# Row statistics from the transposed input, and index weights in other slots of the arena

## The chip, the cores and the metric

The kernel runs on one core of a Trainium2 chip. The metric is the device time of one execution in microseconds (us): the median of three runs is 1517.07 us (1515.85 to 1518.37). The core has an engine for matrix products (TensorE, PE in the views), whose weight loads are listed apart (PEld), VectorE (DVE), ScalarE (ACT), GpSimd (POOL) and SyncE (SP), which issues most transfers. Each engine works through its own list of instructions in order and waits for others by semaphores. SBUF holds the tiles, PSUM the products.

## What is computed

One layer of a streaming encoder on 1024 rows of width 1024 in float32. The start, on which the change bears, is this; the three mixers, the gates and the channel mixer follow and are only named here.

```python
def rms_norm(x, g):
    y = x32 * lax.rsqrt(jnp.mean(x32 * x32, axis=-1, keepdims=True) + EPS)
    return y * g

h = rms_norm(x, g_mix[l])
z = h @ w_in[l]
aq, ak, av, bq, bk, bv, iq, ik, iw, cx, cy, gt = split_cols(z)
q_i = apply_rope(iq, cos, sin)                      # the indexer: 4 heads of 64
k_i = apply_rope(rms_norm(ik, g_idx_k[l]), cos, sin)
dots = jnp.einsum('bqhe,bse->bqhs', qib, ki)
score = jnp.einsum('bqhs,bqh->bqs', jax.nn.relu(dots), wib)
# top 256 keys by score for branch B; y_a, y_b, y_c; gates; w_out; SwiGLU with w_ffn_in, w_ffn_out
```

The mean of squares is over the width of a row, so each of the 1024 rows has one scale.

## The kernel before, in words

Precision is kept by splitting each float32 operand in two parts: `split` (L100) rounds on ScalarE (`hi`, L101) and subtracts on VectorE (`lo`, L102), and `mm3` (L116) makes three products of them (L117 to L119). The normalized input is kept transposed, width on the partitions, as eight pairs of tiles `hTh` and `hTl`, one for each 128 of the width, 1024 rows long.

The rows come in five batches, `BATCH` (L29): one tile of 128 rows, one, and three times two. Per batch the queue of SyncE loads the rows themselves (`x`, 512 KB a tile, L166), for their sums of squares, and the same rows transposed (`xT`, 512 KB each, L172), for the products. Behind the first batch stand the small parameters (`sm`) and the index weights in three pieces of two, three and three chunks (`W0K`, L146, L150); behind the last the rope table (`cs`). These loads are kept in program order. Then, per batch: ScalarE squares each row tile and adds along the row (L187), GpSimd multiplies and adds epsilon (`rs_v`, L126) and raises to the power of -0.5 (`rs_x`, L127), TensorE transposes a broadcast of that column so that the scale of each row lies along the free axis of a PSUM bank (`rb`, L190), and VectorE multiplies eight chunks by gain and scale (L197); each of the eight is split, where the first batch also splits the index weights at chunks 0, 2 and 5. The index projection (L254 to L262) is 24 products for each of eight row tiles, 192 in all, 324 columns each. After four tiles the index keys are normalized (`ssk`, `rsk`), queries and keys are rotated (L279 to L286) and transposed (L291, L295), and for blocks 2 to 7 of 128 queries the scores are made: two products for each head (L242, L243), relu on ScalarE (L310), weighted sums on VectorE (L312, L314). Beside that the first projections of the other branches run (`w_zg`, tiles `wzr`, `wzh`, `wzl`, products of 256 columns in L117 to L119).

Tiles come from two lists of arena slots: `ring` (slots 0 to 6) for weights that stream through, among them the index weights and `w_zg`, and `sl` (slots 7 to 49) for the rest. A slot that was freed goes to the end of its list, and a tile in it waits for the readers of the tile before. What stands where in the list of each engine is decided by a scheduler from the program text and the tiles' dependences; only loads marked as kept in program order, and a string of letters for the work further behind, fix places by hand.

Of the kernel before, what the change touches and what calls it, by code (L numbers as in the profile page):

```python
# [10 lines left out]
F32 = mybir.dt.float32  # L11
F32R = mybir.dt.float32r
I32 = mybir.dt.int32
BF16 = mybir.dt.bfloat16
AF = mybir.ActivationFunctionType
OP = mybir.AluOpType
# [4 lines left out]
D = 1024  # L21
NT = 8
KD = 8
DFF = 2816
NF = DFF // 128
EPS = 1e-6
# [53 lines left out]
def hybrid_kernel(ctx: ExitStack, tc: tile.TileContext, x, xt, small, cs, bias_a, lru_w, w_idx, w_zg, w_c, w_g, w_b,  # L80
                  w_o, w_fi, w_fo, out):
    nc = tc.nc
    V, S, G, PE = nc.vector, nc.scalar, nc.gpsimd, nc.tensor
    const = ctx.enter_context(tc.tile_pool(name="const", bufs=1))
    arena = ctx.enter_context(tc.tile_pool(name="arena", bufs=1))
    dram = ctx.enter_context(tc.tile_pool(name="dram", bufs=1, space=bass.MemoryType.DRAM))
    sl = Slots(arena, range(NRING, NSLOT))
    ring = Slots(arena, range(NRING))
# [7 lines left out]
    def smc(name, j=0, n=1):  # L96
        o, _ = SMALL_OFF[name]
        return sm[:, o + j:o + j + n]

    def split(raw, hi, lo, eng=None):  # L100
        S.activation(hi, raw, AF.Copy)  # L101
        (eng or V).tensor_tensor(lo, raw, hi.bitcast(F32), op=OP.subtract)  # L102
# [13 lines left out]
    def mm3(o, lh, ll, rh, rl, first, last, **kw):  # L116
        PE.matmul(o, lhsT=lh, rhs=rh, start=first, stop=False, **kw)  # L117
        PE.matmul(o, lhsT=lh, rhs=rl, start=False, stop=False, **kw)  # L118
        PE.matmul(o, lhsT=ll, rhs=rh, start=False, stop=last, **kw)  # L119

    mhalf = const.tile([128, 16], F32, name="mhalf")
    V.memset(mhalf, -0.5)

    def rsqrt(dst, src, n, scale):
        v = const.tile([128, n], F32, name="rs_v", tag=f"rsv{n}", bufs=2)
        G.tensor_scalar(v, src, scale, EPS, op0=OP.mult, op1=OP.add)  # L126
        G.tensor_tensor(dst, v, mhalf[:, 0:n], op=OP.pow)  # L127
# [4 lines left out]
    def gbank(shape=(128, 512)):  # L132
        return psum.tile(list(shape), F32, name="G", tag="G", bufs=2)

    def sbank(shape=(128, 1024)):
        return psum.tile(list(shape), F32, name="S", tag="S", bufs=2)

    def tbank(shape=(128, 512)):
        return psum.tile(list(shape), F32, name="T", tag="T", bufs=2)

    ss_x = const.tile([128, NT], F32, name="ss_x")
    rs_x = const.tile([128, NT], F32, name="rs_x")
# [3 lines left out]
    W0K = ((0, 2), (2, 3), (5, 3))  # L146

    def load_w0(k0, kn):
        raw = ring.get((128, kn, 324), F32, "w0r")
        tc.keep_in_program_order(nc.sync.dma_start(raw, w_idx[:, k0:k0 + kn, :]))  # L150
        w0.append([k0, kn, raw])

    def split_w0(q):
        k0, kn, raw = w0[q]
        hi, lo = ring.get((128, kn, 324), F32R, "w0h"), ring.get((128, kn, 324), F32R, "w0l")
        split(raw, hi, lo)
        ring.free(raw)
        w0[q] = (k0, kn, hi, lo)

    xts, parts = [None] * NT, []
    for t0, tn in BATCH:
        for t in range(t0, t0 + tn):
            xts[t] = sl.get((128, D), F32, "x")
            tc.keep_in_program_order(nc.sync.dma_start(xts[t], x[t * 128:(t + 1) * 128, :]))  # L166
        kn = KD // tn
        ps_ = []
        for n in range(tn):
            c0 = 1024 * (t0 + n)  # L170
            pt = sl.get((128, kn, 128 * tn), F32, "xT")
            tc.keep_in_program_order(nc.sync.dma_start(pt.rearrange("p k t -> p (k t)"), xt[:, c0:c0 + 1024]))  # L172
            ps_.append(pt)
        parts.append(ps_)
        if t0 == 0:
            tc.keep_in_program_order(nc.sync.dma_start(sm, small))
            for q in range(len(W0K)):
                load_w0(*W0K[q])
        if t0 == 6:
            ctab = sl.get((128, NT, 2, 64), F32, "cs")  # L180
            tc.keep_in_program_order(nc.sync.dma_start(ctab, cs))
    junk = sl.get((128, D), F32, "junk")
    for (t0, tn), ps_ in zip(BATCH, parts):
        w = 128 * tn
        rb = sbank((128, w))
        for t in range(t0, t0 + tn):
            S.activation(junk, xts[t], AF.Square, accum_out=ss_x[:, t:t + 1])  # L187
        rsqrt(rs_x[:, t0:t0 + tn], ss_x[:, t0:t0 + tn], tn, 1.0 / D)
        for t in range(t0, t0 + tn):
            PE.transpose(rb[:, 128 * (t - t0):128 * (t - t0) + 128], rs_x[:, t:t + 1].to_broadcast([128, 128]), ident)  # L190
        kn = KD // tn
        for k in range(KD):
            if t0 == 0 and k in (0, 2, 5):
                split_w0((k + 1) // 3)
            r = ps_[k // kn][:, k % kn]
            hi, lo = (a[:, 128 * t0:128 * t0 + w] for a in hT[k])
            V.scalar_tensor_tensor(r, r, smc("g_mix", k), rb, op0=OP.mult, op1=OP.mult)  # L197
            split(r, hi, lo)
        sl.free(*xts[t0:t0 + tn], *ps_)
    sl.free(junk)  # L200

    def bc(ap, n):
        a = list(ap.ap)
        return bass.AP(tensor=ap.tensor, offset=ap.offset, ap=[a[0], *a[1:-1], [0, n], a[-1]])
# [44 lines left out]
    for g in range(2):  # L249
        zq = sl.get((128, 4, 4, 64), F32, "zq")  # L250
        zk = sl.get((128, 4, 2, 64), F32, "zk")
        for j in range(4):
            t = 4 * g + j
            p = gbank((128, 324))  # L254
            for k0, kn, wh, wl in w0:
                for k in range(k0, k0 + kn):
                    hh, hl = hT[k]
                    mm3(p, hh[:, 128 * t:128 * t + 128], hl[:, 128 * t:128 * t + 128], wh[:, k - k0], wl[:, k - k0],
                        k == 0, k == KD - 1)
            S.activation(zq[:, j].rearrange("p h d -> p (h d)"), p[:, 0:256], AF.Copy)  # L260
            S.activation(zk[:, j, 0], p[:, 256:320], AF.Copy)
            S.activation(iw[:, t], p[:, 320:324], AF.Copy, scale=1.0 / 16.0)  # L262
        if g == 1:
            for _, _, wh, wl in w0:
                ring.free(wh, wl)
        sq = sl.get((128, 4, 64), F32, "sq")
        S.activation(sq, zk[:, :, 0], AF.Square)
        ssk = const.tile([128, 4], F32, name="ssk", bufs=2)
        V.tensor_reduce(ssk, sq, axis=AX.X, op=OP.add)
        rsk = const.tile([128, 4], F32, name="rsk", bufs=2)  # L270
        rsqrt(rsk, ssk, 4, 1.0 / 64)
        for j in range(4):
            V.scalar_tensor_tensor(zk[:, j, 0], zk[:, j, 0], rsk[:, j:j + 1], smc("gi", 0, 64), op0=OP.mult,
                                   op1=OP.mult)
        sl.free(sq)
        t2 = sl.get((128, 4, 4, 64), F32, "t2")
        ct = ctab[:, 4 * g:4 * g + 4, 0, :]
        st = ctab[:, 4 * g:4 * g + 4, 1, :]
        V.tensor_mul(t2[:, :, :, 0:32], zq[:, :, :, 32:64], bc(st[:, :, 0:32], 4))  # L279
        V.tensor_mul(t2[:, :, :, 32:64], zq[:, :, :, 0:32], bc(st[:, :, 32:64], 4))  # L280
        V.tensor_mul(zq, zq, bc(ct, 4))
        V.tensor_add(zq, zq, t2)
        V.tensor_mul(t2[:, :, 0, 0:32], zk[:, :, 0, 32:64], st[:, :, 0:32])
        V.tensor_mul(t2[:, :, 0, 32:64], zk[:, :, 0, 0:32], st[:, :, 32:64])
        V.tensor_mul(t2[:, :, 1], zk[:, :, 0], ct)
        V.tensor_add(zk, bc(t2[:, :, 0], 2), bc(t2[:, :, 1], 2))  # L286
        c = slice(512 * g, 512 * g + 512)
        for pr in range(2):
            pt = tbank((128, 4, 128))
            for j in range(4):  # L290
                PE.transpose(pt[:, j], zq[:, j, 2 * pr:2 * pr + 2].rearrange("p h d -> p (h d)"), ident)  # L291
            stack(pt.rearrange("p a b -> p (a b)"), qi[2 * pr][:, c], qi[2 * pr + 1][:, c])
        pt = tbank((128, 4, 128))
        for j in range(4):
            PE.transpose(pt[:, j], zk[:, j].rearrange("p h d -> p (h d)"), ident)  # L295
        pk = pt.rearrange("p a b -> p (a b)")
        S.activation(kih[:, c], pk, AF.Copy)
        V.tensor_sub(kil[:, c], pk, kih[:, c].bitcast(F32))
        sl.free(zq, zk, t2)
# [4 lines left out]
    for i in range(2, NT):  # L304
        w = (i + 1) * 128
# [965 lines left out]
    ring = Slots(arena, fore + rw.free_list + rr.free_list + sl.free_list[:9])  # L1271
# [242 lines left out]
```

## Time and profile before

| | before |
|---|---|
| median of 3 runs | 1517.07 us (1515.85 to 1518.37) |
| profiled execution, its time | 1517.05 us |
| its span | 1515.3 us |
| PE busy | 1469.1 us, 97% of the span |
| VectorE busy | 1119.1 us, 74% |
| ScalarE busy | 762.9 us, 50% |
| GpSimd busy | 109.5 us, 7% |
| TensorE's mean granted clock | 0.994 |

The span is the profiled work from its first to its last instruction; 1.75 us lie around it. A busy share is a mean over stages with different limits, so a stage is read from its own stretch. Times in the views are us from the start of the span. A line of the timeline is one instruction or a run of equal ones: start, time, engine, line, operation, what is written and read, shape, count, and in brackets how long the engine had waited before it and for what. A matmul's time includes its passage through the array; how often one starts is the distance of the starts.

### The profile page before, as it was taken

What the parts mean: (1) busy time and instruction counts of PE and PEld (TensorE: products, weight loads), DVE (VectorE), ACT (ScalarE), POOL (GpSimd) and SP (SyncE); (2) the same over time, 40 slices, a digit from 0 to 9 for tenths busy, and PEclk for the clock granted to TensorE, in tenths of its full rate; (3) what the DMA queues carried; (4) which work ended last, traced back from release to release, by engine and by line L of the source; (5) the groups of instructions that cost most, each with busy time, mean ns of one, the idle gap of its engine ahead of it and who ended that gap; (6) DMA issues with size and microseconds to landing.
All of it is one profiled execution on the core that took longest, in us unless ns stands there. A gap on an engine that the chain in (4) does not pass through costs nothing.

```text
span 1515.3 us, 19935 instructions
## 1 busy us (share of the span) xinstructions
PE 1469.1 (97%) x7556; PEld 1228.5 (81%) x7556; DVE 1119.1 (74%) x1985; ACT 762.9 (50%) x1208; POOL 109.5 (7%) x161
## 2 busy tenths in 40 slices
PE   6999899999999998999999989999999999999999
PEld 5898688989788876788888868888888888888887
DVE  7989999869666779767889776555555556578972
ACT  6557768775778656443214663333333333344340
POOL 1220011210000200110000200000000000000000
PEclk9999999999999999999999999999999999999999
DMA  7011212122111121357552412323232323697532
GB/s 289 29 46 54 87 32 102 39 70 85 56 53 45 42 102 53 125 181 298 216 189 75 153 59 96 111 97 112 98 111 98 111 97 126 230 386 263 190 125 89
DMA packets 52240, 182.59 MB, mean 120 GB/s; under 512 B 6000, under 2 KB 6128, under 8 KB 52144
## 3 DMA queue, kind: packets, MB, share of 16 engines
q1 hardware_dynamic: 38448, 135.17, 25.9%
q0 software_dynamic: 11968, 43.00, 7.2%
q10 hardware_dynamic: 1728, 3.15, 0.5%
q8 instruction: 59, 0.97, 0.3%
q14 instruction: 37, 0.30, 0.1%
HBM read 135.94 MB, written 45.35 MB: 120 GB/s over the span
## 4 chain that ended last, share of the span: by engine, by line
PE 75%; DVE 14%; ACT 5%; issue 3%; DMA 2%; POOL 0%; POOLq 0%; ACTq 0%; SPq 0%; DVEq 0%
PE B L119 15%; PE B L118 15%; PE B L117 15%; PE G L118 7%; PE G L119 7%; PE G L117 6%; DVE key L643 3%; PE T L426 2%; PE T L118 1%; PE T L117 1%; PE T L119 1%; PE T L418 1%; PE S L117 1%; PE S L118 1%; PE S L119 1%
## 5 line engine op out<-in xcount | busy, mean ns | idle before, releaser
L118 PE MATMUL B<-hl,fwh 128*128 128x512 f32 x528 | 205.8, 392 | 1.5 <-DVE hl L1026 1.5
L117 PE MATMUL B<-hh,fwh 128*128 128x512 f32 x528 | 203.4, 393 | 1.6 <-ACT hh L1025 1.3
L119 PE MATMUL B<-hh,fwl 128*128 128x512 f32 x528 | 198.8, 391 | 1.9 <-DVE fwl L102 1.9
L117 PEld LDWEIGHTS B<-hh,fwh 128*128 128x128 f32 x528 | 99.8, 189 | 23.5 <-ACT hh L1025 2.2
L119 PEld LDWEIGHTS B<-hh,fwl 128*128 128x128 f32 x528 | 99.8, 189 | 23.1 <-DVE fwl L102 2.3
L118 PEld LDWEIGHTS B<-hl,fwh 128*128 128x128 f32 x528 | 99.8, 189 | 22.9 <-DVE hl L1026 2.2
L118 PE MATMUL G<-wzl,hTh 128*128 128x256 f32 x384 | 111.3, 290 | 5.3 <-DVE wzl L102 5.3
L117 PE MATMUL G<-wzh,hTh 128*128 128x256 f32 x384 | 110.8, 291 | 1.3 <-ACT wzh L101 0.6
L119 PE MATMUL G<-wzh,hTl 128*128 128x256 f32 x384 | 110.8, 289 | 0.0
L102 DVE TENSOR_TENSOR fwl<-s,fwh 128x1024 fp32r<-128x1024 f32 x44 | 53.7, 1223 | 74.1 <-PE B L118 74.1
L118 PE MATMUL B<-fol,foh 128*128 128x512 f32 x264 | 102.9, 390 | 0.0
L119 PE MATMUL B<-foh,fol 128*128 128x512 f32 x264 | 101.9, 389 | 0.0
L117 PE MATMUL B<-foh,foh 128*128 128x512 f32 x264 | 101.1, 389 | 0.0
L655 ACT ACTIVATE junk_s<-score,ngS 128x1024 int8<-128x1024 f32 (+2 forms) x78 | 77.5, 994 | 17.5 <-DVE ngS L653 13.5
L118 PEld LDWEIGHTS G<-wzl,hTh 128*128 128x128 f32 x384 | 74.6, 194 | 7.1 <-DVE wzl L102 6.1
L119 PE MATMUL G<-hTh,wgl 128*128 128x512 f32 x192 | 75.8, 395 | 2.0 <-DVE wgl L102 2.0
L117 PEld LDWEIGHTS G<-wzh,hTh 128*128 128x128 f32 x384 | 74.6, 195 | 3.2 <-ACT wzh L101 1.1
L117 PE MATMUL G<-hTh,wgh 128*128 128x512 f32 x192 | 75.8, 395 | 0.0
L118 PE MATMUL G<-hTl,wgh 128*128 128x512 f32 x192 | 75.4, 393 | 0.0
L119 PEld LDWEIGHTS G<-wzh,hTl 128*128 128x128 f32 x384 | 74.8, 195 | 0.3 <-issue 0.2
L101 ACT ACTIVATE fw<-fb 128x512 fp32r<-128x512 f32 x22 | 13.9, 632 | 117.0 <-PE B L119 117.0
L101 ACT ACTIVATE foh<-fa 128x1024 fp32r<-128x1024 f32 x33 | 35.0, 1061 | 57.5 <-DMA fa<-pd 37.7
(486 smaller groups left out, 3847.7 us busy)
## 6 DMA issues: line engine op xcount, KB each, us to landing
fw<-in_w_fo SPq DMA_DIRECT2D x33, 512.0 KB, 5.7
fa<-pd SPq DMA_DIRECT2D x33, 512.0 KB, 5.5
gl<-gd SPq DMA_DIRECT2D x24, 512.0 KB, 5.9
fa<-in_w_fi SPq DMA_DIRECT2D x22, 512.0 KB, 3.5
fb<-in_w_fi SPq DMA_DIRECT2D x22, 512.0 KB, 3.6
pd<-act POOLq DMA_DIRECT2D x22, 512.0 KB, 5.3
ga<-in_w_g SPq DMA_DIRECT2D x18, 512.0 KB, 3.6
x<-in_x SPq DMA_DIRECT2D x16, 512.0 KB, 5.9
```

What stands on the lines that cost most here:

```text
L101: S.activation(hi, raw, AF.Copy)
L102: (eng or V).tensor_tensor(lo, raw, hi.bitcast(F32), op=OP.subtract)
L117: PE.matmul(o, lhsT=lh, rhs=rh, start=first, stop=False, **kw)
L118: PE.matmul(o, lhsT=lh, rhs=rl, start=False, stop=False, **kw)
L119: PE.matmul(o, lhsT=ll, rhs=rh, start=False, stop=last, **kw)
L418: PE.transpose(pt[:, b - c0], P[:, 128 * b:128 * b + 128], ident)
L426: PE.matmul(o[64 * e:64 * e + 64, :], lhsT=v[(b0 + b) // 4][:, (b0 + b) % 4, h, :], rhs=PT[e][:, b, :], start=b == 0, stop=b == nb - 1, sk ...
L643: V.tensor_scalar(o[:, 0:(i + 1) * 128], (keys or score)[i], ap[:, j:j + 1], 0.0, op0=op, op1=OP.add, accum_out=self.cnt[:, j:j + 1])
L655: S.activation(junk_s[:, 0:(i + 1) * 128], score[i], AF.Sign, bias=self.ng.bitcast(F32)[:, j:j + 1], accum_out=self.cnt[:, j:j + 1])
```

## The change

The row tiles `x` and their loads in the prologue are gone. Each `xT` tile is squared on ScalarE into a tile `sq` of the same size, and TensorE adds the squares over the partitions: for each row tile eight float32 products, the squares as weights (128x128), a column of ones as the moving side, into a bank of PSUM. VectorE scales this and adds epsilon on its way out of PSUM, and GpSimd only takes the power. The index weights (raw tiles and both parts) take slots of `sl` and no longer of `ring`. Lines behind the change lie 7 further down.

```diff
     def load_w0(k0, kn):
-        raw = ring.get((128, kn, 324), F32, "w0r")
+        raw = sl.get((128, kn, 324), F32, "w0r")
...
         k0, kn, raw = w0[q]
-        hi, lo = ring.get((128, kn, 324), F32R, "w0h"), ring.get((128, kn, 324), F32R, "w0l")
+        hi, lo = sl.get((128, kn, 324), F32R, "w0h"), sl.get((128, kn, 324), F32R, "w0l")
         split(raw, hi, lo)
-        ring.free(raw)
+        sl.free(raw)
...
-    xts, parts = [None] * NT, []
+    parts = []
     for t0, tn in BATCH:
-        for t in range(t0, t0 + tn):
-            xts[t] = sl.get((128, D), F32, "x")
-            tc.keep_in_program_order(nc.sync.dma_start(xts[t], x[t * 128:(t + 1) * 128, :]))
         kn = KD // tn
...
-    junk = sl.get((128, D), F32, "junk")
+    ones = const.tile([128, 1], F32, name="ones")
+    V.memset(ones, 1.0)
     for (t0, tn), ps_ in zip(BATCH, parts):
         w = 128 * tn
+        kn = KD // tn
         rb = sbank((128, w))
-        for t in range(t0, t0 + tn):
-            S.activation(junk, xts[t], AF.Square, accum_out=ss_x[:, t:t + 1])
-        rsqrt(rs_x[:, t0:t0 + tn], ss_x[:, t0:t0 + tn], tn, 1.0 / D)
+        sums = tbank((128, tn))
+        sqs = []
+        for pt in ps_:
+            sq = sl.get((128, kn, w), F32, "sq")
+            S.activation(sq, pt, AF.Square)
+            sqs.append(sq)
+        for t in range(tn):
+            for k in range(KD):
+                PE.matmul(sums[:, t:t + 1], lhsT=sqs[k // kn][:, k % kn, 128 * t:128 * t + 128], rhs=ones,
+                          start=k == 0, stop=k == KD - 1)
+        sl.free(*sqs)
+        V.tensor_scalar(ss_x[:, t0:t0 + tn], sums, 1.0 / D, EPS, op0=OP.mult, op1=OP.add)
+        G.tensor_tensor(rs_x[:, t0:t0 + tn], ss_x[:, t0:t0 + tn], mhalf[:, 0:tn], op=OP.pow)
         for t in range(t0, t0 + tn):
             PE.transpose(rb[:, 128 * (t - t0):128 * (t - t0) + 128], rs_x[:, t:t + 1].to_broadcast([128, 128]), ident)
-        kn = KD // tn
...
-        sl.free(*xts[t0:t0 + tn], *ps_)
-    sl.free(junk)
+        sl.free(*ps_)
...
-                ring.free(wh, wl)
+                sl.free(wh, wl)
```

The order of VectorE's list from the first batch's scale on, before (`xT_102` is the first batch's tile, `xT_113` the second's):

```order
L372 TENSOR_SCALAR ga_824<-sm 128x1
L494 TENSOR_SCALAR hb<-sm 128x8
L495 TENSOR_SCALAR hb<-sm 128x24
L197 SCALAR_TENSOR_TENSOR xT_102<-xT_102,sm,S 128x128 x8
L102 TENSOR_TENSOR w0l_149<-w0r_105,w0h_148 128x648
L102 TENSOR_TENSOR hTl_85<-xT_102,hTh_84 128x128
```

The same place after (`xT_100` is the first batch's tile; `ss_x` is the new instruction that takes the sums out of PSUM):

```order
L379 TENSOR_SCALAR ga_881<-sm 128x1
L501 TENSOR_SCALAR hb<-sm 128x8
L502 TENSOR_SCALAR hb<-sm 128x24
L102 TENSOR_TENSOR w0l_143<-w0r_103,w0h_142 128x648
L102 TENSOR_TENSOR w0l_153<-w0r_105,w0h_152 128x972
L196 TENSOR_SCALAR ss_x<-T 128x1
L102 TENSOR_TENSOR w0l_166<-w0r_107,w0h_165 128x972
L205 SCALAR_TENSOR_TENSOR xT_100<-xT_100,sm,S 128x128 x8
L102 TENSOR_TENSOR hTl_85<-xT_100,hTh_84 128x128
```

The three index splits moved ahead of the first batch's multiplications, and the new instruction stands between the second and the third.

VectorE's list where the third batch begins, before (`xT_119` and `xT_121` are its tiles):

```order
L102 TENSOR_TENSOR hTl_97<-xT_113,hTh_96 128x128
L102 TENSOR_TENSOR hTl_99<-xT_113,hTh_98 128x128
L197 SCALAR_TENSOR_TENSOR xT_119<-xT_119,sm,S 128x256 x4
L197 SCALAR_TENSOR_TENSOR xT_121<-xT_121,sm,S 128x256 x4
L102 TENSOR_TENSOR hTl_85<-xT_119,hTh_84 128x256
L102 TENSOR_TENSOR hTl_87<-xT_119,hTh_86 128x256
```

The same place after (`xT_111` and `xT_113` are the third batch's tiles):

```order
L102 TENSOR_TENSOR hTl_97<-xT_109,hTh_96 128x128
L102 TENSOR_TENSOR hTl_99<-xT_109,hTh_98 128x128
L196 TENSOR_SCALAR ss_x<-T 128x2
L102 TENSOR_TENSOR wzl_892<-wzr_889,wzh_891 128x1024
L102 TENSOR_TENSOR wzl_1118<-wzr_1115,wzh_1117 128x1024
L205 SCALAR_TENSOR_TENSOR xT_111<-xT_111,sm,S 128x256 x4
L205 SCALAR_TENSOR_TENSOR xT_113<-xT_113,sm,S 128x256 x4
L102 TENSOR_TENSOR hTl_85<-xT_111,hTh_84 128x256
L196 TENSOR_SCALAR ss_x<-T 128x2
L102 TENSOR_TENSOR hTl_87<-xT_111,hTh_86 128x256
```

Two differences of `w_zg` now stand ahead of the third batch's multiplications (another stands among the second batch's differences), and the fourth batch's sums are taken out after one difference of the third.

TensorE's list around the transposes of the fourth batch, before (`L190` with x2 is a batch's pair; `w0h`, `w0l` are the index weights' parts):

```order
L117 MATMUL G<-w0h_171,hTh_94 128x324
L119 MATMUL G<-w0h_171,hTl_97 128x324
L190 MATMUL S<-ident,rs_x 128x128 x2
L117 MATMUL G<-w0h_171,hTh_98 128x324
L118 MATMUL G<-w0l_172,hTh_98 128x324
```

TensorE's list after, from the third batch's transposes to the fourth's (`sq_269` and `sq_271` are the fourth batch's squares, `sq_319` and `sq_321` the fifth's; 12 index products stand ahead of the last two rows' transposes):

```order
L193 MATMUL T<-ones,sq_271 128x1
L199 MATMUL S<-ident,rs_x 128x128 x2
L193 MATMUL T<-ones,sq_271 128x1 x3
L193 MATMUL T<-ones,sq_319 128x1 x4
L193 MATMUL T<-ones,sq_321 128x1 x4
L193 MATMUL T<-ones,sq_319 128x1 x4
L193 MATMUL T<-ones,sq_321 128x1 x4
L118 MATMUL G<-w0l_153,hTh_90 128x324
L119 MATMUL G<-w0h_152,hTl_91 128x324
L199 MATMUL S<-ident,rs_x 128x128 x2
L117 MATMUL G<-w0h_152,hTh_92 128x324
```

Before, 16, 32, 85 and 98 of the 192 index products stood ahead of the transposes of batches 1 to 4 (counted from 0); after, 10, 10, 12 and 30.

## Rows read from the trace of the kernel before

**Rows 1.** The page's part 1 (busy us, share of span) and part 4 (chain).

```profile
PE 1469.1 (97%) x7556; PEld 1228.5 (81%) x7556; DVE 1119.1 (74%) x1985; ACT 762.9 (50%) x1208; POOL 109.5 (7%) x161
...
PE 75%; DVE 14%; ACT 5%; issue 3%; DMA 2%; POOL 0%; POOLq 0%; ACTq 0%; SPq 0%; DVEq 0%
```

**Rows 2.** Stretches: length; busy PE, PEld, DVE, ACT, POOL; clock, DMA share, GB/s.

```profile
0.00:25.00 25.00, 14.46 (x68) 12.57 (x69) 16.85 (x66) 17.12 (x47) 5.13 (x15) 1.00 0.94 364
25.00:50.00 25.00, 22.41 (x150) 21.32 (x150) 20.54 (x50) 13.27 (x43) 7.45 (x5) 1.00 0.26 94
...
150.00:200.00 50.00, 41.64 (x242) 33.93 (x241) 48.95 (x169) 33.98 (x68) 1.06 (x2) 0.93 0.21 74
```

**Rows 3.** DMA issues in 0 to 100 us: count, KB, median us to landing.

```profile
x<-in_x SPq DMA_DIRECT2D x8, 512.0 KB, 9.9
xT<-in_xt SPq DMA_DIRECT2D x8, 512.0 KB, 10.2
```

**Rows 4.** Short stretches around the end of the loads, columns as in Rows 2.

```profile
20.00:25.00 5.00, 4.03 (x28) 3.76 (x27) 4.83 (x14) 5.00 (x16) 0.45 (x2) 1.00 1.03 408
25.00:30.00 5.00, 5.00 (x36) 4.99 (x35) 1.82 (x6) 3.07 (x9) 1.58 (x3) 1.00 0.92 365
30.00:35.00 5.00, 4.11 (x26) 3.51 (x24) 5.00 (x14) 4.56 (x16) 0.00 (x0) 1.00 0.01 3
```

**Rows 5.** Timeline of VectorE, 0 to 84 us.

```profile
15.27 2.16 DVE L197 SCALAR_TENSOR_TENSOR xT<-xT,sm,S 128x128 f32<-128x128 f32 x8 [1.62 <-PE S L190]
17.34 1.82 DVE L102 TENSOR_TENSOR hTl<-xT,hTh 128x128 fp32r<-128x128 f32 x8
19.31 3.22 DVE L197 SCALAR_TENSOR_TENSOR xT<-xT,sm,S 128x256 f32<-128x256 f32 x8 [0.15 <-PE S L190]
...
28.65 3.22 DVE L197 SCALAR_TENSOR_TENSOR xT<-xT,sm,S 128x256 f32<-128x256 f32 x8 [3.17 <-PE S L190]
...
38.54 2.76 DVE L102 TENSOR_TENSOR hTl<-xT,hTh 128x256 fp32r<-128x256 f32 x8
41.22 0.68 DVE L280 TENSOR_TENSOR t<-zq,cs 128x512 f32<-128x512 f32 x1
...
53.33 1.23 DVE L102 TENSOR_TENSOR wzl<-wzr,wzh 128x1024 fp32r<-128x1024 f32 x1
...
75.07 0.62 DVE L312 TENSOR_SCALAR score<-relu,iw 128x768 f32<-128x768 f32 x1 [0.45 <-ACT relu L310]
```

**Rows 6.** Timeline of ScalarE, 0 to 10 us.

```profile
4.33 1.06 ACT L187 ACTIVATE junk<-x 128x1024 f32<-128x1024 f32 x1 [2.31 <-DMA x<-in_x]
```

**Rows 7.** Timeline of GpSimd, 0 to 50 us.

```profile
27.29 0.19 POOL L126 TENSOR_SCALAR rs_v<-ss_x 128x2 f32<-128x2 f32 x1 [1.60 <-ACT junk L187]
27.57 0.69 POOL L127 TENSOR_TENSOR rs_x<-rs_v,mhalf 128x2 f32<-128x2 f32 x1
37.10 4.86 POOL L126 TENSOR_SCALAR rs_v<-ssk 128x4 f32<-128x4 f32 x1 [8.85 <-DVE ssk L269]
```

**Rows 8.** Timelines of TensorE's weight loads, 57 to 59.3 and 150 to 160 us.

```profile
57.25 0.46 PEld L295 LDWEIGHTS T<-ident,zk 128*128 128x128 f32 x4
...
151.70 0.41 PEld L426 LDWEIGHTS T<-PT,v 128*64 128x64 f32 x6 [0.35 <-issue]
```

**Rows 9.** Timeline of TensorE, 0 to 75 us.

```profile
14.27 0.47 PE L119 MATMUL G<-w0h,hTl 128*128 128x324 f32 x1
14.54 0.47 PE L117 MATMUL G<-w0h,hTh 128*128 128x324 f32 x1
...
16.34 0.31 PE L117 MATMUL G<-w0h,hTh 128*128 128x324 f32 x1
16.49 0.31 PE L118 MATMUL G<-w0l,hTh 128*128 128x324 f32 x1
...
48.27 1.03 PE L291 MATMUL T<-ident,zq 128*128 128x128 f32 x8
...
54.61 0.39 PE L118 MATMUL G<-wzl,hTh 128*128 128x256 f32 x1 [2.20 <-DVE wzl L102]
...
69.46 0.44 PE L242 MATMUL S<-kih,qi 128*128 128x384 f32 x1 [0.20 <-ACT relu L310]
```

## The prediction

> **What bounds the kernel now.** I read the page's shares first [rows 1]: TensorE is busy 97% of the span and makes up 75% of the chain that ended last, so only its gaps and what stands on its path can pay. The table by stretches says where gaps are [rows 2]: 10.5 us idle in 0 to 25 us, 2.6 in 25 to 50, and 8.4 in 150 to 200, where VectorE is busy 48.95 of 50 us and sets the pace. The change touches only the first 75 us. There the loads come first: xT's tiles of 512 KB take 10.2 us each from issue to landing, as x's eight do [rows 3], and the queue moves 408 GB/s until it has nothing left at about 29.5 us (a share of 0.92 in 25 to 30 us, 0.01 in 30 to 35) [rows 4]. VectorE, which normalizes the five batches of rows, waits 1.62 us before batch 1's multiplications and 3.17 before batch 3's (at 28.65) [rows 5]. So half the x load could go, and these 4.8 us with it. That is what the change can win; what it pays lies in the order of the instructions.
>
> **Removed.** Eight loads of 512 KB are 4,096 of 10,133 KB ahead of and with cs; at 408 KB per us the queue is 10.0 us less full. The squares of row tiles on ScalarE (1.06 us for 128x1024 [rows 6]) are replaced by eight squares of the same size, so ScalarE gets no relief. GpSimd's multiply-add per batch (0.19 us [rows 7]) becomes a VectorE instruction on one or two columns; I take 0.1 us, between 0 and the 0.2 of GpSimd, five times.
>
> **Added on TensorE.** 64 sum products, fp32, 128 weights by one column. An fp32 product shows two weight loads (line 426: the order has 264 products, the trace 528 loads). Six loads of 64 columns take 0.41 us, 0.07 each, and four of 128 take 0.46, 0.115 each [rows 8]. So one product costs at least 0.14 us; with the 128 columns that the weights have here 0.23, and 0.46 if all runs at TensorE's lower clock. I take 0.23, by the row with the same columns: 64 x 0.23 = 14.7 us (9 to 29). Nothing below zero is possible, since nothing is taken from TensorE for it. Most of it falls into times in which TensorE waits anyway; the price is in what stands behind it.
>
> **Moved, and queued.** Three facts of the order decide. (a) On TensorE only 10, 10 and 12 of the 192 index products stand ahead of the transposes of batches 1, 2 and 3; before, 16, 32 and 85 did. TensorE takes its list in order, so 180 index products wait for batch 3's transposes, which wait for GpSimd's power. (b) On VectorE the index weights' second split stands ahead of batch 0's scale; and, the index weights having left the ring, three w_zg tiles load right behind cs and their splits (1.23 us each [rows 5]) stand ahead of batch 2's multiplications. (c) Batch 3's scale stands behind batch 2's multiplications and one difference.
>
> Step by step, by VectorE's durations [rows 5]: eight multiplications 2.16 us (128 columns) or 3.22 (256), eight differences 1.82 or 2.76, a w_zg split 1.23 (an index split is smaller). The power takes 0.69 [rows 7], and from its end at 28.26 to the multiplications at 28.65 pass 0.4 us for the transposes.
> Loads: the first tile lands at about 4.3 us, where ScalarE's first square begins [rows 6]; small and index weights, 1,429 KB, stand behind it. The last xT lands 4,608 KB before the old end, at 29.5 - 4,608/400 = 18.0, the third w_zg tile at 29.5 - 2,560/400 = 23.1.
> *Batch 0.* The second index tile is there 943 KB after the first landing, at 6.6; ScalarE's rounding of it, behind a square (1.06 each), and VectorE's split (up to 1.23) put the scale at about 9.8. The third split ends at 11.1, then power and transpose: multiplications at 12.2.
> *Batch 1.* VectorE: 12.2 + 2.16 + 1.82 + 0.1, power and transpose: 17.4. TensorE's transpose also stands behind ten index products that need batch 0's differences (from 14.6) and six sums; at the lower clock 14.6 + 2.7 + 2.8 + 0.4 = 20.5. So 17.4 to 20.5 (before 15.27).
> *Batch 2.* 2.16 + 1.82 + 0.1 + 3.69 later VectorE is free, at 25.2 to 28.3, and not before the third w_zg tile is rounded and split (23.1 + 1.06 + 1.23 = 25.4). Power and transposes: 26.5 to 29.4 (before 19.31).
> *Batch 3.* 3.22 + 0.34 + 0.1 gives the scale at 30.2 to 33.1. Seven differences behind it take 2.4 us, then the power 0.69: transposes at 33.3 to 36.2, multiplications 0.4 later (before 28.65).
>
> The power's wait in batches 2 and 3 is the step that needs a row [rows 7]: the multiply-add that GpSimd issued at 37.10 took 4.86 us, until 41.96, while VectorE ran one instruction behind the other to 41.22 + 0.68 = 41.90 [rows 5]; beside pauses of VectorE the same takes 0.19. I therefore let a power end 0.69 us after VectorE's next pause.
> The Trainium skill has a rule that says otherwise ("SBUF — State Buffer", section "Who interferes with whom"): a VectorE instruction with two SBUF inputs and a GpSimd instruction that reads SBUF exclude each other, by a lock that is held for one whole instruction. By that the power would slip in between two differences, batch 3 would come some 2 us earlier and the kernel end at about 1526; the row of 4.86 us speaks against it, and "GpSimd is not held" below has its case.
>
> From batch 3's transposes on TensorE has 180 index products, 0.15 us apart (16.34 to 16.49 [rows 9]), 26.7 us, and 1.5 for twelve transposes among them (0.13 each, eight in 1.03): they end at 61.5 to 64.4 instead of 48.27. From there to the first product of block 4's scores passed 69.46 - 48.27 = 21.2 us. Of that go 2.2 us of waiting for a w_zg split (54.61), which the early loads remove, and 1.5 for the twelve transposes that now stand earlier: 17.5; up to 1 us more if the pauses for ScalarE's relu (0.20 at 69.46) shrink. So that product comes at 78.0 to 81.9, 8.5 to 12.4 later. From the fifth score block on, the order on all engines is that of before but for swaps of neighbours; VectorE's first step of block 5 (75.07 before) shifts by the same. TensorE and VectorE are full in turn behind it, so the shift reaches the end. The lower end needs the early value of each step at once, so I take 11: 1517.05 + 11 = **1528 us**. The profiled execution (1517.05) lies 0.02 below the median of 1517.07, so nothing is corrected.
>
> **Rivals.**
> *The lower clock lasts: slower still.* At the start the index products come every 0.27 us (14.27 to 14.54), 324 columns at 1.2 GHz, and from 16.34 every 0.15, near 2.4 GHz [rows 9]. The granted clock of that stretch reads 1.00 [rows 2], so the level is read from the spacing. Now TensorE stands still for some 3 us ahead of batch 2's transposes and again ahead of batch 3's. If some 25 to 30 products behind them run at the lower level, they cost 0.12 more each: +3 to +3.6, with sums at 0.46 up to +8; 1532. For it: sums of one column are little work. Against: they keep TensorE issuing between the waits.
> The Trainium skill ("TensorE: Matmul & The Clock Gate", section "What's actually happening") calls the lower clock the default, which activity lifts; the rise at 16.34 agrees.
> *GpSimd is not held.* The power runs between VectorE's instructions and a sum costs 0.14: batch 2 comes 1.1 us earlier, batch 3 another 2.4, with the lower end of batch 1 about 5 less, 1523. For it: 0.69 at 27.57. Against: the 4.86 row.
> *Faster.* The relief of the queue wins. It decides at batch 3: if its multiplications begin before 28.65, VectorE's 3.17 and 1.62 us of waiting are gone and the order costs nothing: 1517.05 - 4.8 = 1512. It would need sums at the low bound and w_zg splits that don't hold VectorE; their place in its order speaks against it.
> *No change.* The shift is absorbed where TensorE waits 8.4 us, in 150 to 200 us [rows 2]: 1517 to 1519. Against: VectorE is busy 48.95 of 50 us there with work that is itself behind the shifted blocks, so these waits move along.
>
> **How the numbers follow.** 0.2%, 3 us, is about what a measurement of this kernel can tell from no change. The forecast has 0.50 (1528, alone 1525 to 1531), the lower clock 0.22 (1532, to 1536), GpSimd not held 0.13 (1523, from 1520), faster 0.07 and no change 0.08. The range of 1520 to 1536 leaves out the last two. Faster 0.07, same 0.08, slower 0.85.
>
> **What will show it.** In the changed profile: multiplications of batch 0 at about 12.2 us, batch 1 at 17 to 20, batch 2 at 26.5 to 29, batch 3 at 34 to 36.5; GpSimd's powers of batches 2 and 3 longer than 0.69 or begun at VectorE's pauses; TensorE waiting for rs_x ahead of both transposes; a last index product at 61 to 65; block 5's first step on VectorE at 84 to 87, and from there to the end the same time as before. I am wrong if batch 3's multiplications begin before 30 us, if a sum costs far from 0.23 us, or if the time behind block 5 changes by over 2 us.

## The result: 15 us slower, and where the profile shows it

The changed kernel takes 1532.89 us (median of 4 runs, 1531.19 to 1533.18) against 1517.72 before: a ratio of 1.0097, 95% interval 1.0085 to 1.0109, or +15.2 us. The forecast was 1528, the range 1520 to 1536. The direction, the place and most of the size came as foreseen; the wait that makes it is another one. One execution of the run e1 below, 1705.91 us at a mean granted clock of 0.808 where its others have 0.99, is left out.

The page of the changed kernel, part 1 (busy us, share of span, count):

```profile
PE 1490.4 (97%) x7684; PEld 1253.8 (82%) x7684; DVE 1120.2 (73%) x1991; ACT 764.9 (50%) x1200; POOL 109.4 (7%) x156
```

TensorE has 128 more instructions and is busy 21.3 us longer than in [rows 1]; the span is 1531.0 us. Stretches (length; busy PE, PEld, DVE, ACT, POOL; clock; DMA share; GB/s):

```profile
0.00:25.00 25.00, 16.28 (x74) 16.20 (x75) 11.43 (x51) 16.64 (x30) 3.20 (x9) 1.00 0.83 311
25.00:50.00 25.00, 25.00 (x130) 24.94 (x131) 19.26 (x51) 11.33 (x32) 5.12 (x3) 1.00 0.00 1
```

The loads are over before 25 us, as the change meant; in 25 to 50 the queue moves 1 GB/s (before 94 [rows 2]). But TensorE, which before had 2.6 us of gaps there, has none now, and VectorE's idle time went from 4.5 to 5.7 us. Timeline of TensorE (start, time, engine, line, operation, count, idle before and for what):

```profile
5.70 3.57 PE L193 MATMUL T<-ones,sq 128*128 128x1 f32 x16 [5.70 <-ACT sq L189]
12.29 0.48 PE L199 MATMUL S<-ident,rs_x 128*128 128x128 f32 x1 [3.02 <-POOL rs_x L197]
...
21.34 9.81 PE L193 MATMUL T<-ones,sq 128*128 128x1 f32 x46
31.02 0.67 PE L199 MATMUL S<-ident,rs_x 128*128 128x128 f32 x2
31.48 8.11 PE L193 MATMUL T<-ones,sq 128*128 128x1 f32 x38
...
40.13 0.63 PE L199 MATMUL S<-ident,rs_x 128*128 128x128 f32 x2
...
42.72 0.44 PE L119 MATMUL G<-w0h,hTl 128*128 128x324 f32 x1
42.99 0.32 PE L117 MATMUL G<-w0h,hTh 128*128 128x324 f32 x1
...
69.79 0.31 PE L119 MATMUL G<-w0h,hTl 128*128 128x324 f32 x1
```

A product of a sum shows as two records. 46 records take 9.81 us, 38 take 8.11: 0.213 each, **0.427 us a product**, near the 0.46 that the forecast named for the case that all runs at TensorE's lower clock. TensorE stands in sums from 21.34 to 39.45 with nothing else between but two transposes. Batch 2's transposes (31.02) and batch 3's (40.13) come when the sums ahead of them in the list are done; there is no idle time before either (two index products stand ahead of batch 3's). The index products start 0.27 us apart until 42.72 and 0.15 behind 42.99, and end at 69.9 instead of 48.3 [rows 9]. VectorE shows the same from the other side:

```profile
12.81 2.16 DVE L205 SCALAR_TENSOR_TENSOR xT<-xT,sm,S 128x128 f32<-128x128 f32 x8 [1.00 <-PE S L199]
...
21.59 2.16 DVE L205 SCALAR_TENSOR_TENSOR xT<-xT,sm,S 128x128 f32<-128x128 f32 x8 [4.41 <-PE S L199]
...
26.48 2.53 DVE L102 TENSOR_TENSOR wzl<-wzr,wzh 128x1024 fp32r<-128x1024 f32 x2
31.72 3.22 DVE L205 SCALAR_TENSOR_TENSOR xT<-xT,sm,S 128x256 f32<-128x256 f32 x8 [2.71 <-PE S L199]
...
35.27 2.43 DVE L102 TENSOR_TENSOR hTl<-xT,hTh 128x256 fp32r<-128x256 f32 x7
39.62 0.16 DVE L196 TENSOR_SCALAR ss_x<-T 128x2 f32<-128x2 f32 x1 [1.92 <-PE T L193]
40.80 3.22 DVE L205 SCALAR_TENSOR_TENSOR xT<-xT,sm,S 128x256 f32<-128x256 f32 x8 [1.02 <-PE S L199]
...
91.94 0.62 DVE L319 TENSOR_SCALAR score<-relu,iw 128x768 f32<-128x768 f32 x1 [0.46 <-ACT relu L317]
```

Every wait of VectorE just ahead of a batch's multiplications is for TensorE (`PE S`). The first step of block 5, 75.07 before [rows 5], is at 91.94, 16.9 later. Behind it 1439.1 us pass to the end of the span, before 1440.2: the shift is carried, 1.1 us come back. That it is carried through the waits of 150 to 200 us shows when that stretch and the next are read 15.75 us later (first the row of 200 to 400 us of the kernel before, then the two of the changed kernel):

```profile
200.00:400.00 200.00, 197.38 (x1291) 171.96 (x1291) 169.66 (x431) 147.29 (x281) 24.05 (x24) 0.99 0.19 63
```

```profile
165.75:215.75 50.00, 41.77 (x240) 33.76 (x239) 48.95 (x171) 33.59 (x68) 1.60 (x3) 0.93 0.21 74
215.75:415.75 200.00, 197.03 (x1296) 170.98 (x1295) 170.41 (x434) 147.88 (x282) 24.09 (x24) 1.00 0.18 62
```

TensorE is busy 41.77 of 50 us and VectorE 48.95, against 41.64 and 48.95 in [rows 2], and 197.03 of the next 200 against 197.38. The gaps moved with the work; none was used up.

### The profile page after: what moved, and what is told of

It is laid out like the page before. It is cut to its first block, busy times and chain, and to the rows that moved or that the text cites. A ratio compares the mean times of both kernels' runs of the same rounds, so it can differ in the third digit from the quotient of the medians.

```text
span 1531.0 us, 20152 instructions
## 1 busy us (share of the span) xinstructions
PE 1490.4 (97%) x7684; PEld 1253.8 (82%) x7684; DVE 1120.2 (73%) x1991; ACT 764.9 (50%) x1200; POOL 109.4 (7%) x156
## 4 chain that ended last, share of the span: by engine, by line
PE 78%; DVE 13%; ACT 5%; issue 2%; DMA 2%; SPq 0%; POOL 0%; ACTq 0%; DVEq 0%
PE B L119 15%; PE B L118 14%; PE B L117 14%; PE G L118 7%; PE G L119 7%; PE G L117 7%; DVE key L650 3%; PE T L433 2%; PE T L193 1%; PE T L118 1%; PE T L119 1%; PE T L117 1%; PE T L425 1%; PE S L249 1%; PE S L117 1%
## 5 line engine op out<-in xcount | busy, mean ns | idle before, releaser
L662 ACT ACTIVATE junk_s<-score,ngS 128x1024 int8<-128x1024 f32 (+2 forms) x78 | 77.5, 993 | 17.5 <-DVE ngS L660 13.4
L1229 DVE TENSOR_TENSOR act<-act,B 128x512 f32<-128x512 f32 x22 | 15.1, 688 | 65.7 <-PE B L119 65.7
```

Of the source, the lines that this page charges most:

```text
L662: S.activation(junk_s[:, 0:(i + 1) * 128], score[i], AF.Sign, bias=self.ng.bitcast(F32)[:, j:j + 1], accum_out=self.cnt[:, j:j + 1])
L1229: V.tensor_add(a1, a1, x)
```

## The experiments

Two theories. **T**: the shift comes from the sum products, 0.427 us each at the lower clock, that stand in TensorE's list ahead of the transposes of batches 2 and 3. **D**: it comes from VectorE and GpSimd, that is, from the w_zg splits ahead of batch 2's multiplications (which the free ring made possible) and the power that VectorE holds up, the step on which the forecast was built.

From the first step of block 5 to the end of the span it is 1438 to 1446 us in the kernels below, before 1440.2. So the end of a run carries between 2 us less and 6 us more that the prologue's rows don't explain, and the verdicts go by those rows first. The rows are those of one execution each; e8's (1525.88 us) is the fastest of its five and lies 4.3 us under their median.

| kernel | median us | ratio (95%) | batch 3's multiplications | first step of block 5 |
|---|---|---|---|---|
| before | 1518 | | 28.65 | 75.07 |
| changed | 1532.89 | 1.0097 (1.0085 to 1.0109) | 40.80 | 91.94 |
| e1 slots only | 1516.30 | 0.9992 (0.9982 to 1.0001) | 29.04 | 75.06 |
| e2 ring back | 1539.68 | 1.0141 (1.0126 to 1.0156) | 40.18 | 94.93 |
| e3 one-pass sums | 1519.58 | 1.0010 (1.0001 to 1.0020) | behind batch 2's (29.22) | 81.43 |
| e4 idle products | 1541.13 | 1.0150 (1.0135 to 1.0165) | 40.80 | 93.71 |
| e5 extra sums | 1536.10 | 1.0119 (1.0102 to 1.0136) | 33.76 | 93.11 |
| e6 half the sums | 1525.26 | 1.0052 (1.0037 to 1.0067) | 32.27 | 80.05 |
| e7 sums in rows, root | 1523.92 | 1.0037 (1.0024 to 1.0050) | 33.61 | 80.41 |
| e8 sums in a row | 1530.22 | 1.0077 (1.0064 to 1.0091) | behind batch 2's (26.38) | 79.69 |
| e9 e8, ring | 1522.49 | 1.0031 (1.0020 to 1.0042) | 30.74 | 81.12 |
| e10 e8, order held | 1522.04 | 1.0029 (1.0017 to 1.0041) | 31.94 | 76.77 |
| e11 e10, ring | 1526.86 | 1.0058 (1.0046 to 1.0071) | 32.20 | 78.78 |

**e1: the slots alone.** The kernel before with the slots of the change:

```diff
-        raw = ring.get((128, kn, 324), F32, "w0r")
+        raw = sl.get((128, kn, 324), F32, "w0r")
...
-                ring.free(wh, wl)
+                sl.free(wh, wl)
```

> The kernel before with only the index weights moved to the other slots; row tiles and their sums as before. Theory T (the shift of 15 us comes from the 64 sum products, which ran at TensorE's lower clock, 0.427 us each, ahead of the transposes of batches 2 and 3): the prologue has the order of before, so 1516 to 1520. Theory D (the w_zg splits on VectorE and GpSimd's held power set the shift, which the free ring made possible): a good part of the shift is here too, 1521 to 1527.

Nothing: 1516.30, and the first step of block 5 at 75.06. Moving the index weights does no harm by itself; the loss is in the other part or in both together. The run says less on D than its expectation meant: with the loads of `x` still there, the first w_zg split stands behind batch 3's multiplications and not ahead of batch 2's (VectorE):

```profile
40.19 1.22 DVE L102 TENSOR_TENSOR wzl<-wzr,wzh 128x1024 fp32r<-128x1024 f32 x1
```

What splits ahead of batch 2 do is left to e2.

**e2: the ring back.** The changed kernel with that edit undone.

> The changed kernel with the index weights back in the ring, so that no w_zg split stands ahead of batch 2's multiplications; TensorE's list is that of the changed kernel. T: batch 2's transposes still wait for 22 sum products behind batch 1's, so its multiplications come at 31 to 32 us as in the changed kernel, 1531 to 1536 (the wait of 2.2 us for a w_zg split may come back). D: three splits of 1.23 us are gone from VectorE ahead of batch 2, 3.7 us, 1527 to 1530.

No w_zg split stands ahead of batch 2 now, and TensorE's list around the sums is that of the changed kernel but for one product. Rows of TensorE:

```profile
20.73 9.39 PE L193 MATMUL T<-ones,sq 128*128 128x1 f32 x44
29.98 0.67 PE L199 MATMUL S<-ident,rs_x 128*128 128x128 f32 x2
```

of GpSimd and of VectorE:

```profile
25.27 0.70 POOL L197 TENSOR_TENSOR rs_x<-ss_x,mhalf 128x2 f32<-128x2 f32 x1 [8.80 <-DVE ss_x L196]
```

```profile
30.68 3.22 DVE L205 SCALAR_TENSOR_TENSOR xT<-xT,sm,S 128x256 f32<-128x256 f32 x8 [5.49 <-PE S L199]
```

The power is done at 25.97, in its usual 0.70 us, and still the transposes wait until the 44 records are through, 4 us. VectorE's wait grew from 2.71 to 5.49 us: what the splits filled before is now idle. Batch 2 starts 1.0 us earlier (0.3 ahead of T's 31 to 32), batch 3 0.6. D expected 3.7 and falls; T holds at these rows. The time went past T's 1536: the first w_zg split now stands at 68.10, the first step of block 5 comes 3.0 us later than in the changed kernel, and 4 more are lost behind it. So within the changed kernel the second part of the change is a help.

**e3 and e6: the same sums for half the price, and half the sums.** In e3 squares and ones are in the one-pass format (`F32R`):

```diff
...
-            sq = sl.get((128, kn, w), F32, "sq")
+            sq = sl.get((128, kn, w), F32R, "sq")
...
-                PE.matmul(sums[:, t:t + 1], lhsT=sqs[k // kn][:, k % kn, 128 * t:128 * t + 128], rhs=ones,
+                PE.matmul(sums[:, t], lhsT=sqs[k // kn][:, k % kn, 128 * t:128 * t + 128], rhs=ones,
...
```

> The changed kernel with the squares and the ones rounded to the one-pass format (fp32r, two columns of ones, one read), so a sum product is one weight load and one product in place of two; the sums are a little less exact. T: a sum costs half, 0.21 us, 13.7 us of TensorE go; batch 3's multiplications come at least 6 us earlier than 40.8, 1520 to 1527. D: sums are not what is waited for, 1531 to 1533.

In e6 the loop takes every second chunk, which leaves half of each sum out, and the factor behind it is doubled:

```diff
-            for k in range(KD):
+            for k in range(0, KD, 2):
                 PE.matmul(sums[:, t:t + 1], lhsT=sqs[k // kn][:, k % kn, 128 * t:128 * t + 128], rhs=ones,
...
```

> The changed kernel with only every second of the eight products of a row tile, 32 in place of 64 (the scale is then of half the width: part of the computation is left out). T: 32 x 0.427 = 13.7 us of TensorE go, batch 3's multiplications come at 30 to 34 in place of 40.8, 1520 to 1526. D: 1531 to 1533.

Each leaves 64 records in place of 128, and both come close at the first step of block 5: 81.43 and 80.05, 10.5 and 11.9 us earlier than in the changed kernel, of 13.7 us taken from TensorE. e3's time lies just under T's interval, e6's in it, 5.7 us apart by what lies behind block 5 (1438.6 and 1443.7 us). VectorE in e6 (batch 2's multiplications, then batch 3's first run):

```profile
29.06 3.22 DVE L205 SCALAR_TENSOR_TENSOR xT<-xT,sm,S 128x256 f32<-128x256 f32 x8 [0.69 <-PE S L199]
...
32.27 2.04 DVE L205 SCALAR_TENSOR_TENSOR xT<-xT,sm,S 128x256 f32<-128x256 f32 x5
```

The three w_zg splits still stand ahead of batch 2 here. But the order is no longer the changed kernel's: GpSimd takes both powers before batch 2's multiplications. So these runs show what the sums cost; they don't show what the changed kernel's own order would give with cheap sums.

**e5: sums alone, added to the kernel before.** Row tiles, squares on ScalarE and the ring stay; TensorE gets 64 products whose results nobody reads:

```diff
         rsqrt(rs_x[:, t0:t0 + tn], ss_x[:, t0:t0 + tn], tn, 1.0 / D)
+        sums = tbank((128, tn))
+        for t in range(tn):
+            for k in range(KD):
+                PE.matmul(sums[:, t:t + 1], lhsT=ps_[k * tn // KD][:, k % (KD // tn), 128 * t:128 * t + 128], rhs=ones,
+                          start=k == 0, stop=k == KD - 1)
```

> The kernel before, with row tiles, sums on ScalarE and ring as they were, and 64 fp32 products by a column of ones added on TensorE whose results nobody reads (weights are the xT tiles themselves, so that a batch's multiplications wait for its products). T: each costs 0.427 us while the lower clock lasts; 54 of them stand ahead of 169 of the 192 index products, so the time rises by 10 to 20 us, 1528 to 1538, though nothing on GpSimd, in the slots or in the loads has changed. D: within 3 us of 1517.9.

+18 us, inside T's interval, with the first step of block 5 at 93.11, later than in the changed kernel. GpSimd, slots and loads are those of before. TensorE:

```profile
21.16 4.89 PE L194 MATMUL T<-ones,xT 128*128 128x1 f32 x32
...
33.51 6.83 PE L194 MATMUL T<-ones,xT 128*128 128x1 f32 x32
```

and the stretches around these rows:

```profile
20.00:22.00 2.00, 2.00 (x18) 2.00 (x17) 0.54 (x3) 1.46 (x4) 0.34 (x2) 1.00 1.02 406
22.00:24.00 2.00, 2.00 (x17) 2.00 (x17) 0.00 (x0) 0.13 (x1) 0.55 (x1) 0.82 1.04 410
24.00:42.00 18.00, 18.00 (x85) 18.00 (x86) 12.91 (x35) 8.69 (x25) 0.88 (x2) 0.50 0.31 124
42.00:44.00 2.00, 2.00 (x10) 2.00 (x10) 2.00 (x6) 2.00 (x7) 0.00 (x0) 0.56 0.00 0
44.00:46.00 2.00, 2.00 (x16) 2.00 (x15) 2.00 (x7) 0.61 (x3) 0.00 (x0) 1.00 0.00 0
```

Here TensorE came into the sums at the upper clock, from index products 0.15 us apart. Within the first 32 records the granted clock fell to 0.50, though TensorE was busy without a gap; the mean record took 0.15 us, the later ones 0.213. It stayed at 0.50 while sums ran and came back at 42 to 44 us, among the index products that follow at 40.52. So the clock fell while nothing but sums ran, and 0.213 us a record is the 1.2 GHz level. The 0.82 of 22 to 24 us puts the fall near 23.3; some 12 of the 32 records fit behind it at 0.213, so the 20 ahead of it took about 0.11 each, 0.21 us a product. That is an estimate from these rows, and close to the forecast's 0.23.

**e4: idle wide products against the lower clock.**

```diff
+    dum = sl.get((128, 512), BF16, "dum")
+    V.memset(dum, 0.0)
+    for _ in range(18):
+        PE.matmul(gbank(), lhsT=dum[:, 0:128], rhs=dum, start=True, stop=True)
+    sl.free(dum)
```

> The changed kernel with 18 idle products of 512 columns (bf16 zeros, never read): eight ahead of the first sums, the others between the sums of the first batches. T, if the lower clock is only a matter of never having risen: sums from about 12 us on cost 0.21 us in place of 0.427, batch 2's transposes wait for GpSimd's power (28.3) in place of the sums, batch 3's come 5 us earlier, 1525 to 1529. T, if sums let the clock drop: the idle products cost time on top, 1533 to 1537. D: 1533 to 1537.

TensorE at the start, and before the last sums:

```profile
1.23 3.59 PE L144 MATMUL G<-dum 128*128 128x512 bf16 x8 [1.23 <-DVE ones L185]
5.84 3.57 PE L198 MATMUL T<-ones,sq 128*128 128x1 f32 x16 [1.02 <-ACT sq L194]
...
31.64 7.68 PE L198 MATMUL T<-ones,sq 128*128 128x1 f32 x36
```

The idle products did not raise the clock: they start 0.427 us apart for 512 columns each, the lower level, and the sums take 0.213 us a record to their end. It shows no warmed sums, and so says nothing on what they would cost there. The first step of block 5 is 1.8 us later than in the changed kernel, T's second case; another 7 us are lost far behind it (the last attention product starts at 620.7 instead of 612.0), which put the time past T's 1537.

**e7: sums on every partition.** Ones as 128x128 weights and the squares as the moving side, 40 products in all; ScalarE's root and VectorE's reciprocal take the place of power and transposes:

```diff
-        for t in range(tn):
-            for k in range(KD):
-                PE.matmul(sums[:, t:t + 1], lhsT=sqs[k // kn][:, k % kn, 128 * t:128 * t + 128], rhs=ones,
-                          start=k == 0, stop=k == KD - 1)
+        for k in range(KD):
+            PE.matmul(sums, lhsT=ones, rhs=sqs[k // kn][:, k % kn], start=k == 0, stop=k == KD - 1)
...
+        S.activation(rb, sums, AF.Sqrt, scale=1.0 / D, bias=eps)
+        V.reciprocal(rb, rb)
```

> The sums the other way round: a 128x128 tile of ones as weights, the squares (rounded to the one-pass format) as the moving side, eight products of 128 or 256 columns per batch, 40 in all; every partition gets the sum, ScalarE takes the root, VectorE the reciprocal, no GpSimd power and no transposes in the normalization. TensorE has 64 x 128 columns to stream, 6.8 us at 1.2 GHz in place of 27. T: batch 3's multiplications at 26 to 30 us, 1512 to 1520. D (what counts is VectorE's list, where w_zg splits still stand ahead of batch 3's multiplications and the reciprocals come on top): 1522 to 1530.

The time is D's, and here VectorE does set the pace. Its rows, and the stretch of 25 to 50 us:

```profile
10.40 0.95 DVE L201 RECIPROCAL rb<-rb 128x128 f32<-128x128 f32 x1
...
19.68 1.75 DVE L201 RECIPROCAL rb<-rb 128x256 f32<-128x256 f32 x1
```

```profile
25.00:50.00 25.00, 16.21 (x99) 15.94 (x99) 24.21 (x51) 12.78 (x40) 2.09 (x2) 0.86 0.00 0
```

TensorE is busy 16.21 of 25 us and waits 8.8 us at one place; VectorE has 24.21. The wait is put down to ScalarE's copy of index products out of PSUM (`iw`), and the copies of that group had themselves waited, 3.02 and 0.68 us, for VectorE's differences. Two of the three reciprocals of 1.75 us stand between batch 2's multiplications and batch 3's. With cheap sums the bound goes over to VectorE; T, which expected 1512 to 1520, has no say there.

**e8 to e11: a cheap sum with power and transposes kept.** One column of ones as weights, so that the sums stand in one row; ScalarE copies it, and TensorE makes columns of it:

```diff
+        for k in range(KD):
+            PE.matmul(row, lhsT=ones[:, 0:1], rhs=sqs[k // kn][:, k % kn], start=k == 0, stop=k == KD - 1)
...
+        S.activation(rowv[0:1], row, AF.Copy)
+        sums = tbank((128, tn))
+        for t in range(tn):
+            PE.matmul(sums[:, t:t + 1], lhsT=rowv[0:1, 128 * t:128 * t + 128], rhs=one[0:1, 0:1], start=True, stop=True)
```

> The changed kernel with cheap sums: one column of ones (one-pass format) as weights, the squares as the moving side, so the sums of a batch stand in one row; ScalarE copies the row and TensorE turns it into columns with products of one partition; from there as in the changed kernel (VectorE's scale, GpSimd's power, transposes). Sums are 40 products, 6.8 us at 1.2 GHz, and 16 small ones. T: batch 3's multiplications at 27 to 30 us, no long wait of VectorE, 1514 to 1519: the x load comes once for nothing or a small gain, since VectorE's own work from 7 to 42 us leaves at most some 2 us to win. D (GpSimd's held power and the w_zg splits ahead of batch 3): 1521 to 1527.

> The same with the index weights back in the ring: no w_zg split ahead of batch 3 on VectorE, but w_zg comes late again. If the early w_zg tiles are worth something once TensorE is late (the changed kernel was 7 us better with them), 3 to 8 us more than the run before; if they only stood in VectorE's way, 2 to 4 us less.

The sums are cheap; in e8 the eight of a batch of 256 columns are this row:

```profile
22.80 1.07 PE L194 MATMUL T<-sq,ones 128*1 128x256 f32 x8
```

The first step of block 5 comes at 79.69, and yet 4.6 us are missing to before, and the times missed both theories (e8) and the guess on the ring (e9: 7.7 us less than e8 by the medians, 3.4 by the profiled executions). VectorE in e8:

```profile
20.29 2.15 DVE L211 SCALAR_TENSOR_TENSOR xT<-xT,sm,S 128x128 f32<-128x128 f32 x8 [2.47 <-PE S L205]
```

Batch 1 is 5 us later than before (15.27 [rows 5]). The little products that make columns stand in TensorE's list behind index products that wait for batch 0. e10 holds those index products back instead; e9 and e11 are e8 and e10 with the index weights in the ring:

```diff
...
+                    hold = {0: last[1] if k >= 2 else None, 1: last[2], 3: last[4]}.get(t)
+                    with tc.issue_after(hold) if hold is not None else nullcontext():
...
```

where `last` holds the last transpose of the batch that begins at that row tile.

> The cheap sums in a row (as in the run e8), and TensorE's list held near the order of before: of the first row tile's index products all from the third chunk on are issued behind batch 1's transpose, the second tile's behind batch 2's, the fourth's behind batch 4's. If what is left of the shift with cheap sums (5 us at the first step of block 5) is the order in which batches wait for each other, batch 1's multiplications come at 15 to 17 us, batch 2's at 20 to 22, that first step at 74 to 77 us, 1514 to 1519. If it is the longer chain itself (squares, sums, scale, power, transposes by five engines), no change: 79 to 81 us, 1521 to 1526.

> The same with the index weights in the ring, so without early w_zg splits on VectorE. Order: 75 to 78 us at the first step of block 5, 1515 to 1520, up to 2 us more than the run before by the wait for a w_zg split, or up to 3 less where the splits stood in VectorE's way. Longer chain: 79 to 82, 1520 to 1525.

```profile
17.44 2.15 DVE L213 SCALAR_TENSOR_TENSOR xT<-xT,sm,S 128x128 f32<-128x128 f32 x8 [1.85 <-PE S L206]
...
22.57 3.22 DVE L213 SCALAR_TENSOR_TENSOR xT<-xT,sm,S 128x256 f32<-128x256 f32 x8 [1.30 <-PE S L206]
...
76.77 0.62 DVE L329 TENSOR_SCALAR score<-relu,iw 128x768 f32<-128x768 f32 x1 [0.23 <-ACT relu L327]
```

In e10 (rows above) block 5 begins 2.9 us earlier than in e8, 1.7 later than before: most of the rest was order, as its expectation had it. Batches 1 and 2 come 0.4 and 0.6 us behind the interval, and 2.2 and 3.3 later than before. The end, 1522.0, is in the other case's interval; 2.4 us more than before are lost behind block 5, which the prologue doesn't explain. e11's 1526.9 missed both. No version beat the kernel before.

So, at the first step of block 5: 16.9 us in all; 12.3 go when the sums become cheap (91.94 to 79.69, in e8, where the order of the lists moved too), 2.9 with the order of TensorE's list (to 76.77), and 1.7 remain.

## Why the forecast was near, and which step failed

The time lies within the range, but near the upper end, which was drawn for the lower clock and not for the step-by-step sum. That sum came out short: block 4's first product is 16.5 us later than before, forecast 8.5 to 12.4. The forecast's own sign of being wrong, a sum that costs far from 0.23 us, is there; that the time behind block 5 changed by less than 2 us (1.1) is the part that held.

- *Loads.* Right: the queue is empty before 25 us, xT's tiles land 9.4 us after issue, and nothing is won by it.
- *Batch 0* at 12.2: measured 12.81. *Batch 1* at 17.4 to 20.5: 21.59. *Batch 2* at 26.5 to 29.4: 31.72. *Batch 3* at 33.7 to 36.6: 40.80. Each is later than the upper end, and the error grows from batch to batch, as it does when the price of a repeated thing is wrong.
- **The price of a sum is the step that failed.** The text took 0.23 us and kept 0.46 as the end for the lower clock; measured 0.427, two records of 0.213 for each of the 64. 64 x 0.427 = 27.3 us, 12.6 more than the 14.7 of the sum. The row that was chosen (four 128-column loads in 0.46 us) stands among products of w_zg, at the upper clock, and e5 puts a sum at about 0.21 there; in the changed kernel no sum ran at that level.
- **The wait was put down to the wrong engine.** The text let batches 2 and 3 wait for GpSimd's power, held up by VectorE. The power was held up, but that lay beside the sums:

```profile
26.65 1.61 POOL L197 TENSOR_TENSOR rs_x<-ss_x,mhalf 128x2 f32<-128x2 f32 x1 [9.56 <-DVE ss_x L196]
35.43 2.82 POOL L197 TENSOR_TENSOR rs_x<-ss_x,mhalf 128x2 f32<-128x2 f32 x1 [7.17 <-DVE ss_x L196]
```

  They end at 28.26 and 38.25, the transposes come 2.8 and 1.9 us later, at 31.02 and 40.13. So with cheaper sums the power is the next bound, 2 to 3 us before them in each of the two batches. "Most of it falls into times in which TensorE waits anyway" was true only of the first batch's eight products; from 12.29 us on TensorE has no gap ahead of batch 3. The list of the order that the forecast printed showed it: 19 products stand between batch 2's transposes and the first index product behind them. The 23 between batch 1's transpose and batch 2's, and these 19, take 5.3 and 4.4 us at 0.23, and by the forecast's own times they are done before the power; at 0.427 they take 9.8 and 8.1, and are not.
- *The hold.* Batch 3's power ended 0.55 us after VectorE's run of seven differences (35.27 to 37.70), as by the row of 4.86 us [rows 7]. Batch 2's ended at 28.26 while two w_zg splits ran from 26.48 to 29.01: 0.55 us behind the first and ahead of the second's end, so it did not wait for VectorE's pause. That is what the Trainium skill states ("SBUF — State Buffer", section "Who interferes with whom": the lock is held for one instruction); the seven short differences do not agree with it, so the rule and the row are each half right here.
- *From batch 3's transposes on* the working was good: 29.8 us to the end of the index products (28.2 in the sum; 1.2 of the rest is nine products at the lower clock), then 16.1 us to block 4's first product at 85.96 (16.5 to 17.5).
- *Rivals.* The lower clock that lasts is what happened, with its price on the sums rather than on the index products: 1532, +8 with sums at 0.46 had been named. The Trainium skill's reading of that clock ("TensorE: Matmul & The Clock Gate", section "What's actually happening": throttled by default, released by activity) agrees with the return in e5 at 42 to 44 us; the fall there, from 1.00 to 0.50, came while TensorE was busy without a gap. No change fell: the gaps of 150 to 200 us moved along. Faster fell: batch 3 came at 40.80, not before 28.65. "GpSimd is not held" fell with its price of 0.14 a sum; whether the hold itself costs time was not decided, since it lay off the path.
- *Open.* What the changed kernel's own order would cost with sums at 0.23 us was not measured, since every cheaper sum moved the order too; so whether 1528 was the right answer to the assumed price stays open. Why e4, e8 and e11 lose 4 to 6 us behind block 5 stays open; swaps in the order of the lists there are a guess.

## What to carry to other kernels

A sum over the partitions by a column of ones costs a whole weight load per 128x128 tile, twice in fp32 (two records of 0.213 us here), and moves one column: with 64 of them on the engine that bounds the kernel, taking 4 MB off a queue that nothing waits for much is no trade. Where such a sum is needed, the ones on the weight side make it cheap (1.07 us for eight products in e8), though no version here beat the kernel before. Cost each new instruction at both clock levels by asking what stands around it in its own list. When an addition stands ahead of waits in an in-order list, add it up between the waits: that sum, 23 and 19 products here, tells which engine comes last.

## What the runs showed that was not expected

- TensorE's granted clock fell from 1.00 to 0.50 in e5 while the engine was busy without a gap, with nothing but one-column products among the first 32 records. In the changed kernel the records stay 0.213 us apart from 21.34 to 39.45; the rise shows at 42.99, among the index products of 324 columns, whose spacing goes from 0.27 to 0.15 us.
- The granted clock can read 1.00 while the products run at the lower level: this stretch of the changed kernel lies in its sums, with the same 0.213 us a record that e5 shows at 0.50.

```profile
30.00:35.00 5.00, 5.00 (x26) 5.00 (x26) 3.28 (x9) 2.76 (x8) 0.00 (x0) 1.00 0.00 0
```

  In these kernels the spacing of equal products is the better witness from the start to the first rise.
- VectorE's reciprocal takes 0.95 us on 128x128 and 1.75 on 128x256 (e7), where a multiplication of two operands takes 0.27 and 0.40 (2.16 and 3.22 for eight).
